# Recurrence steps queued behind dense products, with new step costs and finer dense pieces, in a two-layer hybrid decoder kernel

## The chip, the core and the metric

The kernel runs on one core of one Trainium2 chip. The metric is the device time of one execution in microseconds, the median over runs; lower is better. The five instruction streams of the core are named as in the profile: PE (TensorE; PEld is its weight loads), DVE (VectorE), ACT (ScalarE), POOL (GpSimd) and SP (SyncE, here only DMA issues).

## The reference

One inference step of a decoder with two layers, for a prompt of 2048 rows and for 8 sequences of 4 new rows each (the 32 sample rows, which bring their own past). Layer 0 is one input projection that feeds 4 heads of HGRN2 (a gated linear recurrence, "A") and 4 heads of forgetting attention ("B", or fox, with a paged cache), then one output projection. Layer 1 is GLA ("C"): the same kind of recurrence with 4 heads, key width 128 and value width 256. Cut to what matters here:

```python
def even_mixer(h, ...):                       # layer 0
    qa, fa, ia, ga, qb, kb, vb, gb, fb = split(h @ w_in)
    f = lb + (1.0 - lb) * sigmoid(fa)
    o_a, s_a = gated_linear_chunked(qa, 1.0 - f, ia, log(f), hgrn_s0)
    o_a = head_rmsnorm(o_a) * silu(ga)
    o_b = fox_attend(qb, kb, vb, log_sigmoid(fb + b)) * silu(gb)
    return concatenate([o_a, o_b]) @ w_out, s_a
def odd_mixer(h, ...):                        # layer 1
    q, k, v, g, r = split(h @ w_in)
    log_f = log_sigmoid(r @ w_gate + b_gate) / 16
    o, s = gated_linear_chunked(q * 128 ** -0.5, k, v, log_f, gla_s0)
    return (head_rmsnorm(o) * silu(g)) @ w_out, s
def step(S, chunk):                           # gated_linear_chunked, per chunk
    b = cumsum(log_f)
    o = (q * exp(b)) @ S + (scores of q and k, decayed by exp(b_t - b_s), causal) @ v
    S = S * exp(b_last) + (k * exp(b_last - b)).T @ v
```

with x + mixer(rmsnorm(x)) around each layer and a last rmsnorm.

## The kernel before

The prompt is worked on in two halves of 1024 rows; the first half (hf 0) carries the 32 sample rows along. The program has three stretches: layer 0 of both halves (to about 850 us of the trace), the attention of B over prompt and cache (to about 1260 us), and layer 1 with both output projections and the final norm.

**Dense work.** A projection is a sum over eight 128-row pieces of the contraction, each piece in three half-precision products (high by high, high by low, low by high; `mm3`, lines 626 to 628). `proj_fm` makes 24 products per result tile in PSUM, `proj_tm` 48 (two row tiles of 24). Each tile is then evacuated by ACT and DVE. The weights arrive by DMA (`wr_...`), and ACT, DVE and POOL scale and split them into halves (`w_...`, lines 356 to 364); `staged` spreads these steps over the units of 256 output columns that are traced.

**Recurrences.** `lin_attn` (line 690) is a generator, called sixteen times: 4 heads by 2 halves by 2 layers. Its parts in order, with the names that the profile shows:
- diagonal scores of 32 rows (`gd_`, L702) and, in hf 0, those of the sample rows (`gds_`, L707);
- the first product of q with the decay f on DVE (L711);
- seven levels w = 1, 2, 4, ... 64: score products on PE (`gl_`, L757; `gls_`, L777, for the sample rows), their way into the scores by DVE or ACT (L768, L764), then q times f on DVE (L789), k times f on POOL (L790) and f times f on DVE (L791). The next level's PE products read the new q and k;
- in hf 0 the `decode` part for the sample rows, put between the levels 4 to 64: `ktS_`, `kpad_`, `oS_` (products with the 8 old states), `stS_` (L841, new states), with the state times its decay on POOL (`s_`, L843) and a sum on DVE (L845);
- transposes of k (`kt_`, L869), states and outputs per chunk (`st_`, `o_`, L897 to L912), splits into two parts for layer 1 (`parts`, L861 on ACT, L862 on DVE or POOL), norm and gate (`finish`, L720 to L740) with the transposes `py_` (L729).

**What sets the order.** The Python program is traced from top to bottom, and a scheduler puts the traced instructions of each engine into one fixed queue, with its own estimate of when each can start; an instruction that is traced later can therefore be ordered earlier. `issue_after(x)` makes what is traced inside it stay behind instruction x in that order. Two generators are woven by `mux(a, ta, b, tb)`: each step yields a cost, and the one with the smaller share of its declared total is advanced. A recurrence is woven with two or three dense units in this way. The declared totals are `LIN_E` (layer 0, per half), `LIN_O` (layer 1) and `LIN3_B` (the last recurrence, woven with the output projection of hf 0); the steps' costs are the numbers that `lin_attn` yields. Layer 1's first three recurrences are also woven with `prep(1)`, which normalizes the rows of the second half (`x1r`: squares on ACT L567, times a gain row on POOL L569, ACT L574, times the row's factor on DVE L575).

## Time and profile before

| | us |
|---|---|
| median of 3 runs | 2328.9 (2323.44 to 2330.65) |
| the profiled execution | 2327.16 |
| its span in the trace | 2325.5 |
| PE busy | 2251.2 (97%) |
| DVE, ACT, POOL busy | 1377.3, 1026.8, 727.0 |
| granted TensorE clock, mean | 0.991 |

The span is what the trace records of the core; the execution's own time is 1.7 us longer. "Busy" counts matmuls until their modelled end, and successive matmuls overlap, so 97% does not mean that 3% is all that could be won. In the table of waits a row names the engine and the instruction that waited, then the engine and instruction that it waited for, and the total, number and longest of these waits. In the timeline a row gives start, duration, engine, line, the tiles written and read, and, in brackets, the idle time ahead of it and what ended it.

In the trace the eight recurrences of layer 0 lie between 95 and 830 us, those of layer 1 between 1470 and 2215 us.

### The profile page before, as it was taken

Reading aid. Unit: us, or ns where it says so; the run is one execution under the profiler, and the core shown is the slowest. Engines: PE = TensorE matmul, PEld = TensorE weight load, DVE = VectorE, ACT = ScalarE, POOL = GpSimd, SP = SyncE. Lnnn points to the kernel's source line nnn. Section 1 sums busy time; section 2 is a strip of 40 time slices with the busy share of each in tenths; the row PEclk is TensorE's granted clock in tenths of the full one; section 3 lists DMA queues with packets and bytes.
Section 4 is the critical chain, followed back from the end, with each engine's and each line's share of the span. In section 5 each row is a group of like instructions: output and inputs, shape, how many; then the busy total and the mean of one; then the engine's idle time right before and its main releaser. Section 6 shows DMA issues by size and latency. Waiting matters only on the chain.

```text
span 2325.5 us, 57677 instructions
## 1 busy us (share of the span) xinstructions
PE 2251.2 (97%) x23060; PEld 1605.5 (69%) x23060; DVE 1377.3 (59%) x3074; ACT 1026.8 (44%) x2264; POOL 727.0 (31%) x780
## 2 busy tenths in 40 slices
PE   7999999999999999999999999999999999999998
PEld 5677678855755876655446888777677666666887
DVE  7756558525653657577767455366665655547554
ACT  6434354211212226456656543545544644554343
POOL 2223424001201214123335445144551432222232
PEclk9999999999999999999999999999999999999999
DMA  7343444755432378876972969424224431115553
GB/s 238 121 126 99 146 135 163 206 137 160 143 120 73 124 187 282 236 248 191 274 257 82 343 193 267 130 79 143 82 93 93 124 92 58 49 56 164 171 186 150
DMA packets 357422, 361.63 MB, mean 156 GB/s; under 512 B 105777, under 2 KB 300658, under 8 KB 353058
## 3 DMA queue, kind: packets, MB, share of 16 engines
q1 hardware_dynamic: 355010, 351.33, 49.3%
q0 software_dynamic: 2144, 6.62, 0.8%
q8 instruction: 181, 2.97, 0.5%
q14 instruction: 87, 0.71, 0.1%
HBM read 244.54 MB, written 96.42 MB: 147 GB/s over the span
## 4 chain that ended last, share of the span: by engine, by line
PE 42%; DVE 2%; POOL 2%; ACT 2%; DMA 1%; issue 1%; SPq 0%; POOLq 0%; DVEq 0%; ACTq 0%
PE pt_o L626 4%; PE pt_o L627 4%; PE pt_o L628 4%; PE pt_Cv L626 2%; PE pt_Cv L628 2%; PE pt_Cv L627 2%; PE gl_C L757 1%; PE o_C L910 1%; PE pt L1449 1%; PE pv L1711 1%; DMA yr<-yT 1%; POOL s_C L843 1%; PE py_C L729 1%; POOL kC L790 0%; PE fo L626 0%
## 5 line engine op out<-in xcount | busy, mean ns | idle before, releaser
L626 PE MATMUL pt_o<-w_o,act 128*128 128x256 f16 x1024 | 279.6, 273 | 2.7 <-ACT sg1C L683 2.7
L627 PE MATMUL pt_o<-w_o,act 128*128 128x256 f16 x1024 | 279.7, 273 | 0.0
L628 PE MATMUL pt_o<-w_o,act 128*128 128x256 f16 x1024 | 279.5, 273 | 0.1
L626 PEld LDWEIGHTS <-act 128*128 128x128 f16 x2304 | 226.3, 98 | 37.4 <-issue 3.7
L627 PEld LDWEIGHTS <-act 128*128 128x128 f16 x2304 | 226.4, 98 | 32.9 <-issue 4.2
L628 PEld LDWEIGHTS <-act 128*128 128x128 f16 x2304 | 226.4, 98 | 30.6 <-issue 2.0
L790 POOL TENSOR_TENSOR kA<-kA,fA 128x512 f32<-128x512 f32 (+1 forms) x56 | 77.2, 1378 | 339.5 <-PE gl_A L757 274.5
L626 PE MATMUL pt_Cv<-w_Cv,act 128*128 128x256 f16 (+1 forms) x512 | 141.4, 276 | 0.0
L627 PE MATMUL pt_Cv<-w_Cv,act 128*128 128x256 f16 (+1 forms) x512 | 141.3, 276 | 0.0
L628 PE MATMUL pt_Cv<-w_Cv,act 128*128 128x256 f16 (+1 forms) x512 | 141.3, 276 | 0.0
L1429 POOL TENSOR_SCALAR L<-L,nm 128x512 f32<-128x512 f32 (+3 forms) x160 | 99.3, 634 | 107.7 <-DVE nm L1425 41.5
L1421 ACT ACTIVATE L<-L,nm,kc 128x512 f32<-128x512 f32 (+3 forms) x160 | 118.2, 740 | 27.7 <-DVE nm L1419 26.9
L790 POOL TENSOR_TENSOR kC<-kC,fC 128x512 f32<-128x512 f32 (+1 forms) x56 | 80.2, 1433 | 142.2 <-PE gl_C L757 100.1
L1456 ACT ACTIVATE th<-pt 128x512 f16<-128x512 f32 (+3 forms) x159 | 81.8, 529 | 92.5 <-PE pt L1449 91.1
L1457 DVE TENSOR_TENSOR tl<-pt,th 128x512 f16<-128x512 f32 (+3 forms) x159 | 95.1, 609 | 21.2 <-ACT th L1456 19.5
L1449 PE MATMUL pt<-ident,L 128*128 128x128 f32 x544 | 91.8, 281 | 1.6 <-POOL L L1429 1.0
L1573 PEld LDWEIGHTS pkt<-ident,pgcache_fox_k 128*128 128x128 f32 x512 | 58.3, 141 | 44.0 <-issue 25.1
L789 DVE TENSOR_TENSOR qC<-qC,fC 128x512 f32<-128x512 f32 (+1 forms) x56 | 73.4, 1311 | 23.4 <-PE gl_C L757 23.4
L1449 PEld LDWEIGHTS pt<-ident,L 128*128 128x128 f32 x544 | 67.6, 144 | 26.1 <-DVE tl L1457 5.2
L1573 PE MATMUL pkt<-ident,pgcache_fox_k 128*128 128x128 f32 x512 | 77.7, 278 | 6.8 <-ACT kts L1577 2.5
L1911 ACT ACTIVATE vC<-pt_Cv,kc 128x512 f32<-128x512 f32 (+1 forms) x40 | 23.9, 599 | 136.5 <-PE pt_Cv L628 136.5
L789 DVE TENSOR_TENSOR qA<-qA,fA 128x512 f32<-128x512 f32 (+1 forms) x56 | 70.1, 1253 | 12.5 <-PE gl_A L757 12.4
(959 smaller groups left out, 6558.2 us busy)
## 6 DMA issues: line engine op xcount, KB each, us to landing
pgcache_fox_k<-in_cache_fox_k SPq DMA_DIRECT2D x128, 256.0 KB, 4.2
pgcache_fox_v<-in_cache_fox_v SPq DMA_DIRECT2D x128, 256.0 KB, 4.1
yr<-yT SPq DMA_DIRECT2D x16, 1024.0 KB, 6.8
x1d<-xo SPq DMA_DIRECT2D x44, 256.0 KB, 3.6
wr_o<-in_w_out_even SPq DMA_DIRECT2D x32, 256.0 KB, 5.1
xo<-in_x_prompt SPq DMA_DIRECT2D x32, 256.0 KB, 5.6
wr_Cv<-in_w_in_odd SPq DMA_DIRECT2D x32, 256.0 KB, 3.5
x1r<-x1d SPq DMA_DIRECT2D x16, 512.0 KB, 4.2
```

The lines of the kernel that those rows point to most:

```text
L626: nc.tensor.matmul(ps, lh[0], rh[0], start=first, stop=False)
L627: nc.tensor.matmul(ps, lh[0], rh[1], start=False, stop=False)
L628: return nc.tensor.matmul(ps, lh[1], rh[0], start=False, stop=last)
L789: nc.vector.tensor_tensor(xv[:, :, 1], xv[:, :, 1], t0.to_broadcast([P, nb, w]), ALU.mult)
L790: nc.gpsimd.tensor_tensor(kv[:, :, 0], kv[:, :, 0], t1.to_broadcast([P, nb, w]), ALU.mult)
L1421: self.last_exp = nc.scalar.activation(lt[:, :w], lt[:, :w], AF.Exp, bias=nm[:, 0:1], scale=ib, accum_out=nm[:, 2 + j : 3 + j])
L1429: nc.gpsimd.tensor_scalar(lt[:, :w], lt[:, :w], nm[:, 1:2], 2.0**14, ALU.mult, ALU.mult)
L1449: nc.tensor.transpose(pt[:, w : w + P], rows[b][s // 4][0][:, (s % 4) * P : (s % 4 + 1) * P], self.ident)
L1456: nc.scalar.activation(th[:, a:w], pt[:, a:w], AF.Copy),
L1457: nc.vector.tensor_tensor(tl[:, a:w], pt[:, a:w], th[:, a:w], ALU.subtract)))
L1573: last = nc.tensor.transpose(pk[:, j * P : (j + 1) * P], pgs[j][:, h * P : (h + 1) * P], self.ident)
L1911: r = nc.scalar.activation(v[h][:, g : g + cnt], ps[:, :, :256], AF.Copy, scale=c)
```

## The change

Four things are altered together.

1. `beside_dense` takes the place of `mux` where a recurrence is woven with dense units. Each step of the recurrence is traced inside `issue_after` on the last product of the dense group traced so far (`self.dense_mm`), so that none of the step's instructions may be ordered ahead of it.
2. While `beside_dense` runs, `proj_fm` and `proj_tm` hand back control every twelve products or every 6 (`proj_fm` after 6, 12, 18 and 24 products of its 24; `proj_tm` after each 12 of its 48) instead of after each tile. These handbacks are of the type `Piece`, which `staged` passes on without counting them among the tiles that trigger its weight steps.
3. The costs that `lin_attn` yields are new: 2000 instead of 1000 behind `gd_`; 200 instead of 1000 behind a level's products and a new 2800 behind its three multiplications; 15000 instead of 5000 as the total of the levels against the decode part; 1200 instead of 440 behind `kt_` of layer 0; about 1000 behind each group of `st_` and `o_`.
4. The declared totals follow: `LIN_E` (20000, 15000) to (42300, 35500), `LIN_O` (31000, 23000) to (55500, 45000), `LIN3_B` 27000 to 52800.

The core of the diff:

```diff
-LIN_E = (20000.0, 15000.0)
-LIN_O = (31000.0, 23000.0)
-LIN3_B = 27000.0
+LIN_E = (42300.0, 35500.0)
+LIN_O = (55500.0, 45000.0)
+LIN3_B = 52800.0
...
+class Piece(float):
+
+    pass
...
     def proj_fm(...):
             ps = pps.tile([P, 512], F32, tag="pj", name=f"pf_{nm}{c0}")
+            full = 24 * (n / 2.4 + 3)
             for k in range(KT):
-                self.mm3(...)
+                self.dense_mm = self.mm3(...)
+                if self.fine and k in (1, 3, 5):
+                    yield Piece(full / 4)
             evac(ps[:M, :n], c0, n)
-            yield 24 * (n / 2.4 + 3)
+            yield full / 4 if self.fine else full
...
     def proj_tm(...):
                 for k in range(KT):
-                    self.mm3(...)
+                    self.dense_mm = self.mm3(...)
+                    if self.fine and (k == KT // 2 - 1 or k == KT - 1 and j + 1 < len(grp)):
+                        yield Piece(12 * 110)
             evac(ps[:n, : len(grp)], g, len(grp), n)
-            yield 24 * len(grp) * 110
+            yield (12 if self.fine else 24 * len(grp)) * 110
...
     def lin_attn(...):
         nc.vector.copy_predicated(dg, self.mdiag.unsqueeze(1).to_broadcast([P, 8, 32]), ps)
-        yield 1000
+        yield 2000
...
-                yield 1000
+                yield 200
                 if hf == 0 and w <= 2:
...
                 nc.vector.tensor_tensor(t1, t1, t0, ALU.mult)
+                yield 2800
...
-            yield from mux(decode(), DEC, levels(LEVELS[2:]), 5000.0)
+            yield from mux(decode(), DEC, levels(LEVELS[2:]), 15000.0)
...
-                yield 440
+                yield 1200
...
-            yield cpb * (1.25 if split else 1.7) * dv
+            yield 1000
...
-                yield (2.95 if split else 3.4) * dv
+                yield 1000 if split else 900
...
-                drain(mux(lin(0), LIN_E[hf], dense(3, 5), 2 * cost))
+                drain(self.beside_dense(lin(0), LIN_E[hf], dense(3, 5), 2 * cost))
...
+    def beside_dense(self, lin, t, dense, td):
+
+
+        def pinned():
+            while True:
+                with self.tc.issue_after(self.dense_mm.ins):
+                    c = next(lin, None)
+                if c is None:
+                    return
+                yield c
+
+        self.fine = True
+        yield from mux(pinned(), t, dense, td)
+        self.fine = False
...
-            for n, c in enumerate(us[j][1](self.ready.pop(j))):
+            n = -1
+            for c in us[j][1](self.ready.pop(j)):
+                if isinstance(c, Piece):
+                    yield c
+                    continue
+                n += 1
...
-                return mux(lins[hf](h), LIN_O[hf], dense(a, a + 3), 66000.0)
+                return self.beside_dense(lins[hf](h), LIN_O[hf], dense(a, a + 3), 66000.0)
...
-            drain(mux(lins[1](3), LIN3_B, third(), 88000.0))
+            drain(self.beside_dense(lins[1](3), LIN3_B, third(), 88000.0))
```

No instruction of work is added or taken away; the change moves instructions within the queues. Line numbers after it are 5 to 11 higher in these functions (L711 is then L721, L790 is L800, L843 is L854).

In the order of the queues the recurrences of layer 0's second half and of layer 1's second half, the last one excepted, stand almost as before. The four of each first half and the last one are moved. Two places follow.

POOL, first recurrence of layer 1 (`kC` is k times f for a level, its form gives the level: 128x128x4 is w = 4; `s_C` is an old state times its decay). Before:

```order
L790 TENSOR_TENSOR kC_21384<-kC_21384,fC_21484 128x128x4
L843 TENSOR_TENSOR s_C_22051<-s_C_22051,fC_21484 128x512
L843 TENSOR_TENSOR s_C_22053<-s_C_22053,fC_21484 128x512
L843 TENSOR_TENSOR s_C_22169<-s_C_22169,fC_21484 128x512
L843 TENSOR_TENSOR s_C_22171<-s_C_22171,fC_21484 128x512
L790 TENSOR_TENSOR kC_21384<-kC_21384,fC_21484 128x64x8
L790 TENSOR_TENSOR kC_21384<-kC_21384,fC_21484 128x32x16
```

After:

```order
L800 TENSOR_TENSOR kC_21384<-kC_21384,fC_21484 128x128x4
L854 TENSOR_TENSOR s_C_22101<-s_C_22101,fC_21484 128x512
L854 TENSOR_TENSOR s_C_22103<-s_C_22103,fC_21484 128x512
L800 TENSOR_TENSOR kC_21384<-kC_21384,fC_21484 128x64x8
L854 TENSOR_TENSOR s_C_22219<-s_C_22219,fC_21484 128x512
L854 TENSOR_TENSOR s_C_22221<-s_C_22221,fC_21484 128x512
L800 TENSOR_TENSOR kC_21384<-kC_21384,fC_21484 128x32x16
```

The k multiplication of level 8 moves ahead of the second pair of decays. The same is found in the second and third recurrence of layer 1. On PE the products of level 8 and of level 16 (`gl_C`) are then separated by 34 dense products of `pt_Cv` with a `stS_C` and the second half of `oS_C`; before, by 17 of them, two `stS_C` and ten of the short sample products `pS_Cv`.

DVE, second recurrence of layer 1, from the diagonal scores (L703, after it L713) to the first level (L768, then L778). `w_Cg` is a weight split, `sg1C` the gate of the dense unit before, `rst_n` and `x1r` belong to the normalization of rows, `scTs` takes `gds_C`, and `qC` with 128x1056 is the first product with f. Before:

```order
L703 COPY_PREDICATED dg<-mdiag,gd_C_23012 128x256
L357 SCALAR_TENSOR_TENSOR w_Cg_23360<-wr_Cg_22804,kc,w_Cg_23360 128x512 x2
L685 SCALAR_TENSOR_TENSOR sg1C_22924<-th_C_23008,sg1C_22924 128x352
L431 TENSOR_SCALAR rst_n_23111<-nss_23109 128x1
L431 TENSOR_SCALAR rst_n_23486<-nss_23484 128x1
L708 COPY_PREDICATED scTs_880<-mdiag,gds_C_23116 32x128
L711 TENSOR_TENSOR qC_22342<-qC_22342,fC_22574 128x1056
L575 SCALAR_TENSOR_TENSOR x1r_22812<-x1r_22812,rsr_n_23113 128x1024
L575 SCALAR_TENSOR_TENSOR x1r_23106<-x1r_23106,rsr_n_23488 128x1024
L768 COPY_PREDICATED dg<-mlev_819,gl_C_23120 128x128
```

After:

```order
L713 COPY_PREDICATED dg<-mdiag,gd_C_23025 128x256
L362 SCALAR_TENSOR_TENSOR w_Cg_23376<-wr_Cg_22850,kc,w_Cg_23376 128x512 x2
L695 SCALAR_TENSOR_TENSOR sg1C_22937<-th_C_23021,sg1C_22937 128x352
L718 COPY_PREDICATED scTs_880<-mdiag,gds_C_23086 32x128
L721 TENSOR_TENSOR qC_22312<-qC_22312,fC_22519 128x1056
L436 TENSOR_SCALAR rst_n_23168<-nss_23166 128x1
L436 TENSOR_SCALAR rst_n_23460<-nss_23458 128x1
L778 COPY_PREDICATED dg<-mlev_819,gl_C_23090 128x128
```

The first product with f moves ahead of the two `rst_n`, and the two `x1r` products move behind the first level. On PE, in the first three recurrences of layer 1, `gds_C` then stands 24 dense products behind `gd_C` (before 48), and the first `gl_C` 36 behind `gds_C` (before 34), so that the first level comes 22 products earlier.

More of the change, by code (lines that the diff above doesn't have):

```diff
@@ L147, in consts @@
         nc.vector.memset(self.mhalf, -0.5)
-        self.col = col
+        self.col, self.fine = col, False
         self.g_even = col("g_even", i["norm_even"][0], KT)
```

14 lines of the change are left out of this document (7 added, 7 removed).

## The prediction

> **What bounds the kernel now.** I read the busy times first, then the waits of PE, then the stretches, and last the timeline at each wait. PE sets the end. This is its line on the profile's page:
>
> ```profile
> PE 2251.2 (97%) x23060; PEld 1605.5 (69%) x23060; DVE 1377.3 (59%) x3074; ACT 1026.8 (44%) x2264; POOL 727.0 (31%) x780
> ```
>
> The change adds no product, so it can act on the time only through the moments in which PE has nothing to do or switches between kinds of products. The windows of the stretches show where these moments are (columns: window, its length, then busy time and count of each engine, granted clock, DMA):
>
> ```profile
> 95.00:430.00 335.00, 328.72 (x4113) 244.32 (x4112) 211.15 (x455) 131.62 (x314) 111.86 (x87) 0.99 0.42 134
> 500.00:830.00 330.00, 329.37 (x3652) 210.96 (x3651) 176.29 (x416) 73.40 (x193) 48.80 (x43) 1.00 0.39 124
> 850.00:1260.00 410.00, 383.65 (x2685) 222.19 (x2683) 288.87 (x918) 232.68 (x539) 143.58 (x263) 0.98 0.75 231
> 1470.00:1840.00 370.00, 359.77 (x4254) 261.56 (x4253) 227.26 (x404) 194.69 (x404) 154.06 (x119) 0.99 0.35 102
> 2120.00:2215.00 95.00, 90.50 (x1213) 77.95 (x1212) 58.03 (x104) 34.66 (x82) 26.86 (x22) 0.98 0.59 187
> ```
>
> PE idles 0.6 us beside the four recurrences of layer 0's second half, 6.3 beside those of its first half, 10.2 beside the four of layer 1's first half and 4.5 beside the last one. The attention's 26 us are in a stretch where no recurrence runs. So about 21 us are all that the edit can reach, and these are its waits, from the list of PE's waits (total, times, longest):
>
> ```profile
> PE gl_C L757 <- POOL kC L790: 5.6, 4, 1.8
> PE pt_o L626 <- ACT sg1C L683: 2.7, 1, 2.7
> PE gl_C L757 <- DVE qC L711: 1.9, 1, 1.9
> PE pt_Bk L626 <- DVE Bvs L1071: 1.9, 1, 1.9
> PE o_C L626 <- ACT pd_C01s L861: 1.6, 1, 1.6
> PE kt_C L869 <- ACT scT L764: 1.4, 1, 1.4
> PE stS_A L841 <- DVE kpad_A L818: 1.3, 1, 1.3
> PE gl_A L757 <- POOL kA L790: 0.7, 1, 0.7
> ```
>
> **Step 1, the k multiplication behind four decays.** POOL in the first recurrence of layer 1, and PE around the level that waits for it, from the timeline:
>
> ```profile
> 1538.78 1.72 POOL L790 TENSOR_TENSOR kC<-kC,fC 128x512 f32<-128x512 f32 x1
> 1540.46 5.28 POOL L843 TENSOR_TENSOR s_C<-s_C,fC 128x512 f32<-128x512 f32 x4
> 1545.70 1.14 POOL L790 TENSOR_TENSOR kC<-kC,fC 128x512 f32<-128x512 f32 x1
> ```
>
> ```profile
> 1541.44 0.74 PE L757 MATMUL gl_C<-qC,kC 128*32 128x16 f32 x64
> ...
> 1543.78 0.27 PE L627 MATMUL pt_Cv<-w_Cv,act 128*128 128x256 f16 x1
> 1543.89 0.27 PE L628 MATMUL pt_Cv<-w_Cv,act 128*128 128x256 f16 x1
> ...
> 1546.89 0.72 PE L757 MATMUL gl_C<-qC,kC 128*32 128x16 f32 x63 [1.74 <-POOL kC L790]
> ```
>
> Level 8's products are over at 1542.2, but POOL works on decays until 1545.74 and finishes the k of that level at 1546.84. PE had run out of other work 1.74 us earlier. The same happens in the second and third recurrence (the waits of these three make 5.2 of the 5.6). With the multiplication ahead of the second pair of decays, POOL is free at 1540.46 + 2 × 1.32 = 1543.1, so the new k is there at 1544.3, about 2.5 us earlier. On PE the next level comes later instead: dense products start 0.11 apart (1543.78 to 1543.89), 34 of them now lie between the two levels and take 3.7 us beside the state products. Arrival moves from 1545.1 to about 1546.5, and the wait is gone with some 2 us to spare. A wait costs a little more than its idle time, since the product ahead is counted until its modelled end, 0.27 after its start, while the next would have started after 0.11: 0.16 each. Gain: 5.2 + 3 × 0.16 = **5.7 us**. The second pair of decays is now late by one multiplication, 1.1 us; who waits for it is the sum on DVE (L845) and a store, not PE. Cover for the level after it (16): both pairs lie ahead of its multiplication as before, and the fourth recurrence keeps its wait of 0.4. Bounds: nothing gained if other work in the new places delays POOL by over 2 us, and 5.9 at most.
>
> **Step 2, the first level comes 22 dense products earlier** in these three recurrences, 22 × 0.11 = 2.4 us. What it needs is the first product of q with f on DVE. The timeline of DVE in the first, second and third recurrence, and POOL in the second:
>
> ```profile
> 1521.34 2.67 DVE L685 SCALAR_TENSOR_TENSOR sg1C<-th_C,sg1C 128x352 f32<-128x352 f32 x1
> ...
> 1524.00 0.28 DVE L708 COPY_PREDICATED scTs<-mdiag,gds_C 32x128 f32<-32x128 int8 x1
> 1524.19 1.24 DVE L711 TENSOR_TENSOR qC<-qC,fC 128x1056 f32<-128x1056 f32 x1
> ```
>
> ```profile
> 1611.23 2.70 DVE L685 SCALAR_TENSOR_TENSOR sg1C<-th_C,sg1C 128x352 f32<-128x352 f32 x1
> ...
> 1615.14 0.15 DVE L431 TENSOR_SCALAR rst_n<-nss 128x1 f32<-128x1 f32 x1 [1.15 <-ACT nsq L567]
> 1615.21 0.28 DVE L708 COPY_PREDICATED scTs<-mdiag,gds_C 32x128 f32<-32x128 int8 x1
> 1615.41 3.25 DVE L711 TENSOR_TENSOR qC<-qC,fC 128x1056 f32<-128x1056 f32 x1
> ```
>
> ```profile
> 1706.21 2.70 DVE L685 SCALAR_TENSOR_TENSOR sg1C<-th_C,sg1C 128x352 f32<-128x352 f32 x1
> ...
> 1709.09 1.24 DVE L711 TENSOR_TENSOR qC<-qC,fC 128x1056 f32<-128x1056 f32 x1
> ```
>
> ```profile
> 1611.20 2.35 POOL L569 TENSOR_TENSOR x1r<-x1r,grow 128x1024 f32<-128x1024 f32 x1 [0.44 <-ACT nsq L567]
> ...
> 1615.19 2.35 POOL L569 TENSOR_TENSOR x1r<-x1r,grow 128x1024 f32<-128x1024 f32 x1 [0.49 <-ACT nsq L567]
> ```
>
> Beside POOL's x1r multiplication the gate takes 2.70 and the q product 3.25, and they end 0.4 and 1.1 us after POOL does (1613.55, 1617.54); alone the q product takes 1.24. [...]
>
> The gate's operation over all its uses (least, median and longest ns):
>
> ```profile
> L685 DVE SCALAR_TENSOR_TENSOR sg1C<-th_C,sg1C x20: 518/683/2703, 1510.9 to 2135.6; 128x352 f32<-128x352 f32 x12, 128x512 f32<-128x512 f32 x8
> ```
>
> PE in the first recurrence, the sample scores among dense products, and in the second, for its arrival:
>
> ```profile
> 1522.60 0.27 PE L628 MATMUL pt_Cv<-w_Cv,act 128*128 128x256 f16 x1
> 1522.81 0.25 PE L707 MATMUL gds_C<-qC,kC 128*32 128x32 f32 x2
> 1522.99 0.28 PE L626 MATMUL pt_Cv<-w_Cv,act 128*128 128x256 f16 x1
> ...
> 1612.81 0.25 PE L707 MATMUL gds_C<-qC,kC 128*32 128x32 f32 x2
> ```
>
> First recurrence: PE reached the level at 1522.99 + 34 × 0.11 = 1526.7 and will reach it at 1524.3; the q product ends at 1525.4. A wait of 1.0 is new, and the second level's wait of 0.3 for DVE goes. Second: PE arrived at 1616.7 and waited until 1618.7. It will arrive at 1614.3. DVE is done with the gate at 1613.9, and the q product no longer stands behind the second `rst_n`, which waited for ACT until 1615.14. If it starts at 1614.2, a microsecond before POOL's second multiplication, it ends at 1615.4: a wait of 1.2 for 1.9. If it meets it, up to 1618.7, a wait of 4.4. I take 1.3, since nothing ahead of it on DVE waits for ACT any more. Third: in the new order no x1r work stands on POOL there, so the gate takes 0.5 to 0.7 and the product is over before 1709, while PE arrives at 1709.3 (3.1 behind the gate's start, as in the second): nothing. Sum: +1.0 − 0.3 − 0.6 = **+0.1 us**, bounds −1.9 (all waits go) and +8 (rival A).
>
> **Step 3, the last recurrence** is woven with the output projection; its later levels come 3 to 5 us later on PE and its first transposes 6.6 us later. ACT there:
>
> ```profile
> 2162.31 0.72 ACT L362 ACTIVATE wr_o<-wr_o,kc 128x512 f32<-128x512 f32 x1 [4.78 <-DMA wr_o<-in_w_out_odd]
> 2164.50 0.72 ACT L362 ACTIVATE wr_o<-wr_o,kc 128x512 f32<-128x512 f32 x1 [1.47 <-DMA wr_o<-in_w_out_odd]
> 2165.23 0.77 ACT L764 ACTIVATE scT<-gl_C 64x256 f32<-64x256 f32 x2
> ```
>
> The scores' copy stood behind a weight scaling that waited for its transfer. With the transposes 6.6 us later the copy is over before PE comes: **−1.6 us** (1.4 and the 0.16). A weight split on POOL is now ahead of the k of level 16 instead of level 32; its 0.4 us of wait stays. The wait of 2.7 at the start of that stretch (`pt_o` for a gate on ACT) is ahead of the recurrence's first step and stays.
>
> **Step 4, layer 0's first half.** The third recurrence's `stS_A` now stands behind all eight `oS_A` and two dense products, about half of its 1.3 goes; in the fourth, the first level's 0.7 goes, since its products come 1.5 us later. Gain **1.5 us** with the 0.16s. Against that, the fourth's state and output steps move 1 to 4 us later, into the evacuation of `Bk` and `Bv` on DVE, where PE waits 1.9 today; there the waits may shift by 2 either way, and I take 0.
>
> **Step 5, switches.** The order has 17 more changes between dense and recurrence products. Around `gds_C` above the next dense product starts 0.39 after the last one, instead of 0.11, with two products of 32 rows between them: some 0.1 us per switch is lost at most. **+1.5 us**, bounds 0.5 and 3. The wait of `o_C` for `pd_C01s` stays at 1.6: ACT's order there is the same. In the attention, which the edit doesn't touch, a few instructions change place; 0, bounds ±3.
>
> Sum: −5.7 + 0.1 − 1.6 − 1.5 + 1.5 = −7.2 us. Profiled execution 2327.16 − 7.2 = 2320.0. The median of the runs is 1.7 above that execution, so the forecast for the median is 2321.7, rounded to **2321.5 us**.
>
> **Rivals.** A, *the wait only moves to the first level.* The three first levels come 2.4 us earlier, and in the first two the q product meets a POOL multiplication of x1r, which costs it 2.0 more (3.25 against 1.24), while in the third the gate still meets one: waits of 3.0, 4.4 and 1.0 instead of 0, 1.9 and 0, together +6.5 − 0.3 instead of +0.1. The time is then 2321.7 + 6.1 = 2328, no change. For it: DVE is packed there from the weight split to the q product. Against it: fewer x1r steps lie there in the new order.
>
> B, *step 1 gains only half.* POOL's queue is in order; if x1r or a weight split gets between, or PE's other work before level 16 shrinks, each wait falls to 0.9 rather than to 0: −2.9 instead of −5.7, and the time is 2324.5. For it: POOL's k multiplication of 1.72 at 1538.78 shows that it too is lengthened by DVE. Against it: 2 us of margin.
>
> C, *slower: a step that is pinned can't fill a dense wait any more.* Place: layer 0's first half, where DVE is busy 63% (211.15 of 335.00) and the dense tile waits for its evacuation, as `pt_Bk` for `Bvs` does. Today the scheduler may slip a ready recurrence step in front of such a tile; pinned, the step stands behind the stalled product, and its DVE work follows late too. Each time costs the 1.9 of that row. It decides once over four such waits arise beyond today's one: −7.2 + 4 × 1.9 is about 0; with eight of them the time is 2321.7 + 15.2 = 2337. Against it: the recurrences of the second half, whose order is nearly the same, wait only 0.6 us in all, so the even spread is mostly present there already.
>
> D, *the order moves too little to show.* 8 of 16 recurrences hardly move, the others' waits are traded for others of like size: 2328 to 2330.
>
> **How the numbers follow.** This forecast 0.52, A 0.12, B 0.14, C 0.14, D 0.08. About 0.3% (7.0 us) is what a measurement of this kernel can tell from no change, so faster means below 2321.9 and slower above 2335.9. The forecast's own range is 2312 to 2327: the bounds of steps 2, 4 and 5 and the attention's 3 together make 5 to 6 either way, and it reaches further down because the 21 us of waits leave more to gain in places that I set to 0 than there is to lose. Two thirds of it lie below 2321.9: 0.35. B adds a quarter of its chance and A a tenth, 0.05: faster 0.40, and slower 0.12 from C with over seven more waits or with other mishaps of its kind, within 0.3% 0.48. The range for 8 in 10 takes in B, A and D and half of C: 2311 to 2334.
>
> **What would show it.** Right: no `gl_C` wait for `kC` in the first three recurrences of layer 1 (the row falls from 5.6 to about 0.5); `kt_C` for `scT` gone; `gl_C` for `qC` at L721 between 1.5 and 3 us in two waits; PE idle in 1470 to 1840 down from 10.2 to about 5. A shows as the last row with 6 us or more; B as a `kC` row of about 3; C as more and longer waits of `pt_Bk`, `pt_Bv` or `pf_B` for DVE before 430. The forecast fails if a wait outside these places changes by more than 3 us, in the attention above all.

## The result: 0.21% slower, and the profile after

| | before | after |
|---|---|---|
| median of 21 runs each | 2325.93 | 2329.51 |
| lowest and highest | 2320.26 to 2332.46 | 2323.61 to 2336.48 |
| the profiled execution | 2327.16 | 2330.60 |
| its span | 2325.5 | 2328.9 |

The ratio of after to before is 1.0021, with a 95% interval from 1.0013 to 1.0029: about 5 us slower, inside the 0.3% that I had called no change, and clearly not the forecast gain of 7. Ratios here compare undisturbed runs on the same chip, and so need not equal the quotient of the two medians. The changed kernel in a second set of runs, later, gave 1.0035 (1.0023 to 1.0048).

The page's line of busy times after the change:

```profile
PE 2246.7 (96%) x23060; PEld 1603.3 (69%) x23060; DVE 1368.6 (59%) x3074; ACT 1028.0 (44%) x2264; POOL 722.6 (31%) x780
```

PE's work is the same 23060 products. Its idle time rose from 74.3 to 82.2 us. The stretches of the prediction, after (window, length, busy time and count of PE, PEld, DVE, ACT, POOL, clock, DMA):

```profile
95.00:430.00 335.00, 324.46 (x4089) 241.42 (x4087) 208.30 (x453) 131.35 (x313) 111.47 (x87) 0.99 0.42 134
...
1470.00:1840.00 370.00, 360.04 (x4263) 262.51 (x4262) 224.70 (x406) 196.04 (x406) 149.21 (x119) 0.99 0.36 105
2120.00:2215.00 95.00, 92.67 (x1229) 79.17 (x1227) 54.03 (x101) 36.26 (x85) 26.06 (x22) 0.98 0.57 182
```

Beside layer 0's first half PE now idles 10.5 us instead of 6.3. Beside layer 1's first half it idles 10.0 instead of 10.2, where I had expected about 5. Beside the last recurrence it idles 2.3 instead of 4.5, as hoped. The list of PE's waits after the change, for the places of the prediction:

```profile
PE gl_C L767 <- DVE rst_n L436: 3.9, 2, 2.9
PE pt_o L631 <- DVE xo L1889: 3.8, 1, 3.8
...
PE pf_Bg L631 <- DVE Bq L1037: 3.3, 2, 2.0
...
PE pt_Bv L631 <- DVE Bvs L1082: 2.3, 1, 2.3
...
PE zC L1982 <- ACT qC L1996: 1.6, 1, 1.6
...
PE pt_Bk L631 <- DVE Bvs L1082: 1.3, 1, 1.3
...
PE py_C00S L739 <- ACT scT L774: 1.3, 1, 1.3
PE py_C01S L739 <- ACT scT L774: 1.3, 1, 1.3
...
PE gl_A L767 <- POOL kA L800: 1.2, 1, 1.2
PE o_C L631 <- ACT pd_C01s L872: 1.2, 1, 1.2
```

The row that I aimed at, `gl_C` for `kC` with 5.6, is gone altogether; so is `kt_C` for `scT`. In their place stand rows that were not there: `pt_o` for `xo`, `pf_Bg` for `Bq`, `zC`, `py_C00S`, a longer `py_C01S` and a longer `pt_Bv`. (The first row names `rst_n`; the level waits for the q product just ahead of it on DVE, as shown below.)

Where the 3.4 us between the two profiled executions arose follows from the starts of the same dense products in both traces, after minus before:

| at (us) | after − before | since the row above |
|---|---|---|
| 462, behind layer 0's first half | +2.9 | +2.9 |
| 1276, behind the attention | +0.75 | −2.2 |
| 2078, behind seven recurrences of layer 1 | −0.76 | −1.5 |
| 2216, end of the last recurrence | −2.1 | −1.3 |
| 2243, 27 us later | +3.5 | +5.6 |

The first two rows are shaky, because they rest on one profile of the kernel before. Against it the attention is 0.4 to 5.9 us shorter in all sixteen other traces of this case. At 462 the four kernels below whose layer 0 has the old order stand at +1.2 to +2.5 as well, with one stretch more of half clock (3.41 us), and the eight with the changed layer 0, this one among them, at +0.6 to +4.5. So of layer 0's +2.9 only a part, and perhaps little, comes from the change. The last row is firm: from 2216 to 2243 the four other traces in which layer 0 and the last recurrence are both changed (one of them without the pin) lose 5.4 to 6.5, the one with layer 0 undone loses 3.7, and the four with the old last recurrence lose nothing.

So most of step 1's gain was eaten within layer 1, layer 0 lost up to 2.9, and 5.6 were lost just behind the last recurrence, in a place that the prediction did not look at.

**Layer 1, the loss at the recurrences' other end.** POOL in the first recurrence does what step 1 said:

```profile
1537.98 1.71 POOL L800 TENSOR_TENSOR kC<-kC,fC 128x512 f32<-128x512 f32 x1
1539.66 2.65 POOL L854 TENSOR_TENSOR s_C<-s_C,fC 128x512 f32<-128x512 f32 x2
1542.28 1.59 POOL L800 TENSOR_TENSOR kC<-kC,fC 128x512 f32<-128x512 f32 x1
```

The k multiplication runs between the two pairs of decays, and three waits of 1.7 to 1.8 end. At the second recurrence's first level, DVE and POOL:

```profile
1612.89 2.72 DVE L695 SCALAR_TENSOR_TENSOR sg1C<-th_C,sg1C 128x352 f32<-128x352 f32 x1
1615.53 0.28 DVE L718 COPY_PREDICATED scTs<-mdiag,gds_C 32x128 f32<-32x128 int8 x1
1615.73 3.20 DVE L721 TENSOR_TENSOR qC<-qC,fC 128x1056 f32<-128x1056 f32 x1
...
1612.87 4.95 POOL L574 TENSOR_TENSOR x1r<-x1r,grow 128x1024 f32<-128x1024 f32 x2 [0.45 <-ACT nsq L572]
```

POOL's two x1r multiplications, which were 1.6 us apart before, now run back to back for 4.95 us: the small factor between them (`rsr_n`) moved behind, and ACT's squares, for which the second of them waited before (0.49), come earlier. Beside them both the gate (2.72; the median of its 20 uses, in two shapes, is 0.61) and the q product (3.20; the median of eight is 1.23) are long; PE comes 22 products earlier, 2.4 us, and waits 2.9. Two kernels of the experiments bear this out: with finer pieces alone, and in the best version below, the two multiplications are 1.6 us apart again, the q product takes 1.24, and no first level waits over 1.0. Each of DVE's two operations ends only after one of POOL's two: the gate at 1615.61, 0.4 after POOL's first (1615.23), the q product at 1618.93, 1.1 after the second (1617.81). Why DVE takes longer beside POOL there, these runs don't show.

The end of the recurrences on ACT, two rows from the first recurrence and six from the second:

```profile
1560.87 0.72 ACT L367 ACTIVATE wr_Cv<-wr_Cv,kc 128x512 f32<-128x512 f32 x1 [4.04 <-DVE qC L799]
1561.49 0.75 ACT L774 ACTIVATE scT<-gl_C 64x256 f32<-64x256 f32 x2
...
1653.68 0.75 ACT L367 ACTIVATE wr_Cv<-wr_Cv,kc 128x544 f32<-128x544 f32 x1 [5.47 <-DMA wr_Cv<-in_w_in_odd]
1654.34 0.53 ACT L1996 ACTIVATE qC<-pf_C02q,kc 128x352 f32<-128x352 f32 x1
1654.78 1.14 ACT L579 ACTIVATE x1r<-x1r,rsr_n 128x1024 f16<-128x1024 f32 x1
1655.81 0.76 ACT L774 ACTIVATE scT<-gl_C 64x256 f32<-64x256 f32 x2
1657.04 0.75 ACT L367 ACTIVATE wr_Cv<-wr_Cv,kc 128x544 f32<-128x544 f32 x1 [0.47 <-DMA wr_Cv<-in_w_in_odd]
1657.69 0.40 ACT L872 ACTIVATE pd_C01s<-scT 128x256 fp32r<-128x256 f32 x1
```

In the second recurrence a weight scaling waits 5.47 us for its transfer, and behind it on ACT stand an evacuation (`zC` waits 1.6 for it), an x1r step, the score copy (`py_C01S` waits 1.3) and a split (`o_C` waits 1.2). Before, ACT stood still at the same weight for 4.60, and only `o_C` with 1.6 and `py_C01S` with 0.2 felt it. In the first recurrence the score copy for which `py_C00S` waits 1.3 stands behind a weight scaling too, ahead of which ACT idled 4.04. I put this down to the 15000 against which the decode part is paced: the sample rows' norm and transposes are stretched to the end of the recurrence, next to the dense tile's end, so more of PE's work stands behind this moment. The run with 9000 below bears that out for the transposes.

**Layer 0.** ACT around the evacuations of `Bq`, before:

```profile
324.23 1.02 ACT L1025 ACTIVATE Bq<-pf_Bq,kc 128x352 f16<-128x352 f32 x2
```

ACT and DVE after:

```profile
322.26 0.57 ACT L1036 ACTIVATE Bq<-pf_Bq,kc 128x352 f16<-128x352 f32 x1
...
326.83 1.15 ACT L533 ACTIVATE xhl<-ny,rsr_n 128x1024 f16<-128x1024 f32 x1 [2.96 <-POOL rsr_n L438]
...
328.88 0.98 ACT L1036 ACTIVATE Bq<-pf_Bq,kc 128x352 f16<-128x352 f32 x2
...
329.53 1.04 DVE L1037 SCALAR_TENSOR_TENSOR Bq<-pf_Bq,kc,Bq 128x352 f16<-128x352 f32 x2
```

Before, two evacuations of `Bq` ran one behind the other. Now the second stands on ACT behind a normalization of rows, in which ACT is idle for 2.96 us until POOL has its factor, and behind the eight instructions of a recurrence's norm (four squares and their sums, 1.0 us from 327.89 on). PE, which needs the PSUM tile, waits 2.0. At the like place of another recurrence, at 162.6, it waits 1.3; there the evacuation stands behind the norm's instructions alone, and these wait for PE's `o_A`.

**Behind the last recurrence.** The chain that ended last runs there through a load of y, whose row starts at 2224.44:

```profile
2220.71 2.73 DVE act L1846 x4
...
2224.44 7.34 DMA yr<-yT
...
2234.04 0.67 DVE xo L1889
2234.75 0.27 PE pt_o L631
```

The load of the next piece of y waits for a buffer, which is free when DVE has split the piece before. DVE came to that late, because of this operation:

```profile
2213.47 0.75 DVE L1889 SCALAR_TENSOR_TENSOR xo<-pt_o,kc,xo 128x512 f32<-128x512 f32 x1 [7.71 <-DMA xo<-x1d]
```

It waited 7.71 us for a residual tile. SP's issues say why, first after the change, then before:

```profile
2202.16 0.37 SPq L1832 DMA_DIRECT2D yr<-yT  x1
...
2205.35 0.44 SPq L1888 DMA_DIRECT2D xo<-x1d  x1
```

```profile
2196.55 1.71 SPq L1857 DMA_DIRECT2D xo<-x1d  x2
...
2202.73 0.37 SPq L1801 DMA_DIRECT2D yr<-yT  x1
...
2220.09 0.41 SPq L1801 DMA_DIRECT2D yr<-yT  x1
```

Before the change the residual loads stood ahead of the y load in SP's queue. Now the y load stands ahead of one of them: SP held it until 2202.16, issued nothing in the 5.6 us behind the store ahead of it, and the residual load followed at 2205.35, 7 to 9 us later than before. The same operation of DVE before the change, and ACT's first split of the y piece before and after:

```profile
2209.57 0.75 DVE L1858 SCALAR_TENSOR_TENSOR xo<-pt_o,kc,xo 128x512 f32<-128x512 f32 x1 [2.64 <-PE pt_o L628]
```

```profile
2228.70 2.56 ACT L1814 ACTIVATE act<-yr,kc 128x512 f16<-128x512 f32 x4 [6.29 <-DMA yr<-yT]
```

```profile
2231.87 2.56 ACT L1845 ACTIVATE act<-yr,kc 128x512 f16<-128x512 f32 x4 [11.54 <-DMA yr<-yT]
```

DVE's operation is 3.9 us late, the next y load 4.35 us late (2224.44 for 2220.09), and ACT's split of that piece 3.2 us. PE, which before had no idle time from 2215 to 2240, waits 3.8. The lateness is not all of it. In each of the eleven traces in which PE waits at this place, it resumes 2.9 us after ACT's first split of the piece (here 2231.87 and 2234.75). Before, that moment (2231.6) lay only 1.4 us ahead of PE (2232.95). So the y piece's 3.2 us and the 2.1 us that PE itself had gained by then add up, less the 1.4: 3.9, against 3.8 measured.

### The profile page after: what moved, and what is told of

It is laid out like the page before. It is cut to its first block, busy times and chain, and to the rows that moved or that the text cites. A ratio compares the mean times of both kernels' runs of the same rounds, so it can differ in the third digit from the quotient of the medians.

```text
span 2328.9 us, 57652 instructions
## 1 busy us (share of the span) xinstructions
PE 2246.7 (96%) x23060; PEld 1603.3 (69%) x23060; DVE 1368.6 (59%) x3074; ACT 1028.0 (44%) x2264; POOL 722.6 (31%) x780
## 4 chain that ended last, share of the span: by engine, by line
PE 41%; DVE 3%; ACT 2%; DMA 2%; issue 1%; SPq 1%; POOL 0%; POOLq 0%; DVEq 0%; ACTq 0%
PE pt_o L631 4%; PE pt_o L633 4%; PE pt_o L632 4%; PE pt_Cv L631 2%; PE pt_Cv L633 2%; PE pt_Cv L632 2%; PE gl_C L767 1%; PE o_C L921 1%; PE pt L1480 1%; DMA yr<-yT 1%; PE pv L1742 1%; PE py_C L739 1%; PE fo L631 1%; PE fo L632 0%; DMA wr_Cv<-in_w_in_odd 0%
## 5 line engine op out<-in xcount | busy, mean ns | idle before, releaser
L800 POOL TENSOR_TENSOR kA<-kA,fA 128x512 f32<-128x512 f32 (+1 forms) x56 | 77.7, 1388 | 331.4 <-PE gl_A L767 268.7
L800 POOL TENSOR_TENSOR kC<-kC,fC 128x512 f32<-128x512 f32 (+1 forms) x56 | 85.1, 1520 | 131.4 <-PE gl_C L767 92.9
```

The source lines that it names most:

```text
L800: nc.gpsimd.tensor_tensor(kv[:, :, 0], kv[:, :, 0], t1.to_broadcast([P, nb, w]), ALU.mult)
```

## The experiments

The kernel was rebuilt from the changed one with a switch for each stretch of recurrences: `p` pins the steps, `f` makes the dense pieces fine, `c` takes the new costs and totals, `d` the new decode total. With all letters it is the changed kernel, with none its instructions have the order of the kernel before. All of these kernels do the whole computation.

```diff
+PARTS_E = ("pfcd", "pfcd")
+PARTS_O = ("pfcd", "pfcd")
+PARTS_L = "pfcd"
...
-        yield 2000
+        yield 2000 if 'c' in self.parts else 1000
...
-            yield from mux(decode(), DEC, levels(LEVELS[2:]), 15000.0)
+            yield from mux(decode(), DEC, levels(LEVELS[2:]), 15000.0 if 'd' in self.parts else 5000.0)
...
+                if "p" in parts:
+                    with self.tc.issue_after(self.dense_mm.ins):
+                        c = next(lin, None)
+                else:
+                    c = next(lin, None)
...
-        self.fine = True
-        yield from mux(pinned(), t, dense, td)
+        self.fine, self.parts = "f" in parts, parts
+        yield from mux(pinned(), t["c" in parts], dense, td)
```

`PARTS_E` is layer 0 (first half, second half), `PARTS_O` layer 1's first seven recurrences (same), `PARTS_L` the last one. Ratios below are to the kernel before, with 95% intervals; the changed kernel's is 1.0021.

### Which stretch loses

```diff
-PARTS_L = "pfcd"
+PARTS_L = ""
```

> Only the last recurrence (woven with the output projection) goes back to the old weave, costs and whole tiles; everything else is the changed kernel. Theory 1 (the loss arises at the end): the SP queue of the changed kernel has the load of a residual tile xo behind the yr load that waits for stores of y, DVE's evacuations come late, and PE waits 3.8 us at 2231 and then runs 3 us at half rate (1.6 us more). Then that 5.5 us goes, the old waits of the last recurrence (0.4 and 1.4, with what belongs to them 2.1) come back: about 3.4 us below the changed kernel, so level with the kernel before within 1.5 us. Theory 2 (the loss is spread over the recurrences, the end varies by chance): within 1 us of the changed kernel, 3 to 4 us above the one before.

Measured 1.0007 (0.9993 to 1.002). PE's longest wait from 2120 to 2240 us; the two others there, of 0.9 and 0.3, are not for `xo` either:

```profile
PE pt_o L634 <- ACT sg1C L696: 2.2, 1, 2.2
```

By the difference from 1.0021 the last stretch costs 0.14%, 3.3 us. The two intervals overlap, so the ratios alone don't show it; the trace does, in which nothing is lost from 2216 to 2243. Now layer 0:

```diff
-PARTS_E = ("pfcd", "pfcd")
+PARTS_E = ("", "")
```

> All eight recurrences of layer 0 go back to the old weave, costs and whole tiles; layer 1 is that of the changed kernel. Theory 4: the dense tiles of layer 0's first half wait because their evacuations on ACT and DVE stand behind more of the recurrence's work (pf_Bg for Bq 3.3, pt_Bv for Bvs 2.3, first level 1.2 in the changed kernel): 3 to 4.3 us below the changed kernel. Rival: these waits are traded for others in the attention that follows: within 1 us.

Measured 1.0007 (0.9994 to 1.002); `pf_Bg` for `Bq` is gone and the waits of the kernel before are back (`pt_Bk` 1.9, `pt_Bv` 0.8, `stS_A` 1.3). By the same reckoning layer 0 costs another 0.14%, and here the traces don't make it firmer (see the table of starts). With both undone:

```diff
-PARTS_E = ("pfcd", "pfcd")
-PARTS_L = "pfcd"
+PARTS_E = ("", "")
+PARTS_L = ""
```

> The change in layer 1's first seven recurrences alone; layer 0 and the last recurrence as in the kernel before. If the losses of layer 0 (theory 4) and of the end (theory 1) add, it is 6 to 7 us below the changed kernel, that is about 2 us below the one before (ratio 0.999): the three waits for kC are gained (5.7) and some 4 us of it are given back in the new waits of the same recurrences. Rival: the losses are not additive, chance in the attention and at the end decides: ratio 1.0005 or more.

Measured 0.999 (0.9976 to 1.0003). Taken at their middles the three shares add up: layer 1's first seven recurrences win some 2 us, the other two stretches lose 3.3 each. The repeat of the changed kernel itself, with no edit, served to see whether these shares stand on a solid sum:

> The changed kernel itself, beside the same runs of the kernel before as the two that follow. If its first ratio of 1.0021 holds here, the parts taken out one by one (1.0000 to 1.0007) are each worth 0.14 to 0.2%; if it comes at 1.0005 or less, most of these differences lie between the sessions and not in the parts.

It gave 1.0035 (1.0023 to 1.0048), so the loss is real and perhaps larger than the first 0.21%, though the two intervals meet; `xo` waited 4.4 in it. Each share above is therefore known to about 0.15% only, which is its own size.

### What makes the wait behind the last recurrence

In the changed kernel the load of y's second piece is kept behind the residual load:

```diff
+        for n, steps in enumerate(self.y_pieces(hf, layer, act, pool)):
+            if (hf, layer, n) == (1, 1, 1):
+                with self.tc.issue_after(self.xos[1, 2, 6].ins):
+                    steps.pop(0)()
...
-                    nc.sync.dma_start(t[:m, :cnt], src)
+                    self.xos[layer, u, g] = nc.sync.dma_start(t[:m, :cnt], src)
```

> The changed kernel, with one DMA order altered on SP: the load of the second yr piece of the second half is kept behind the load of the residual tile xo of the third output unit. Theory 1: that load is the first link of the chain, so the wait of PE for xo (3.8 us) and the half rate behind it go while the gains in the last recurrence stay: 5.5 us below the changed kernel, 2 us below the one before. Rival: the splits of y on DVE, which stand ahead of the evacuation, are late by themselves, since y is stored later; then the wait stays at 3 us or more and the time within 1 us of the changed kernel, or above it, since yr starts later.

Measured 1.0001 (0.999 to 1.0013). The wait is halved:

```profile
PE pt_o L634 <- DVE xo L1899: 1.9, 1, 1.9
```

DVE's operation no longer waits for a residual tile there but for PE, and no slowing of the clock follows (1.00 from 2215 to 2290 us, against 0.98 in the changed kernel). Measured against PE's own progress, the split of y's piece starts 1.9 us earlier than in the changed kernel. So the late residual load is about half of the wait. Two more edits, to the last recurrence of the changed kernel: new costs without pin and pieces, and pieces alone.

```diff
-PARTS_L = "pfcd"
+PARTS_L = "c"
```

> The changed kernel, but the last recurrence has only the new costs: whole tiles, no pin. On SP the load of the residual tile xo then stands ahead of the yr load again. Theory 1 with theory 6: PE's wait for xo at 2231 falls below 1.5 us and the half rate behind it is gone, while kt_C for scT stays gone: 4 to 5.5 us below the changed kernel, level with the one before or below it. Rival: the new costs alone make DVE late there: the wait stays at 2 us or more.

```diff
-PARTS_L = "pfcd"
+PARTS_L = "f"
```

> The changed kernel, but the last recurrence has only the pieces of twelve: old costs and total, no pin. On SP the yr load then stands ahead of the xo load, as in the changed kernel. If the pieces are the cause of the wait at the end, it is there: PE waits for xo 2 us or more at 2231, ratio 1.001 to 1.003 (the run with the costs alone in this place had 1.0000, the one with neither 1.0007). Rival: the wait needs the new costs too: gone here, ratio below 1.0005.

Costs alone: 1.0000 (0.9984 to 1.0015), a wait of 2.0, though its residual load is ahead of the y load. Pieces alone: 1.0001 (0.9986 to 1.0016), a wait of 1.2, though its residual load is behind. In the run with layer 0 undone the whole change is there and the two loads stand as in the changed kernel, yet the wait was 2.0, too. So neither SP's order nor one part of the change decides alone. What the traces have in common is whether DVE stood still for the residual tile: in the five with 7.4 to 8.1 us of it, PE waited 3.5 to 4.4 there, in all others 2.0 or less.

The other half is the sum told above, less a late residual load. With layer 0 undone, ACT's split is 0.4 us earlier than before the change and PE 3.8 us; less the 1.4 that is 2.0. With costs alone, the split is 1.4 later and PE 2.0 earlier, again 2.0. PE ran into a transfer that had only just been hidden, and what it had gained ahead of this place was lost here.

### Which part of the change harms

New costs and decode total everywhere, without pin and pieces:

```diff
-PARTS_E = ("pfcd", "pfcd")
-PARTS_O = ("pfcd", "pfcd")
-PARTS_L = "pfcd"
+PARTS_E = ("cd", "cd")
+PARTS_O = ("cd", "cd")
+PARTS_L = "cd"
```

> The changed kernel with the new costs and totals alone: nothing pinned, whole tiles of 24 and 48 products. Theory 6: the pieces of twelve do the harm, since a recurrence step is then traced inside a tile, ahead of that tile's evacuation; then pf_Bg for Bq in layer 0 and the wait for xo at 2231 go, and the time is 5 us or more below the changed kernel, below the one before. Rival: the costs do it: ratio about 1.002 as in the changed kernel.

Measured 1.0035 (1.002 to 1.005), against my expectation. The waits are others, and longer:

```profile
PE py_C L742 <- ACT wr_o L370: 4.8, 1, 4.8
PE py_C00S L742 <- ACT scT L777: 3.9, 1, 3.9
```

With whole tiles of 24 or 48 products, I think, the new costs place recurrence steps in large lumps. At any rate the same costs with the pieces, in the kernel without the pin below, come to 1.0005, so the pieces repair more than they harm. Pieces everywhere, all else as before:

```diff
+PARTS_E = ("f", "f")
+PARTS_O = ("f", "f")
+PARTS_L = "f"
```

> The kernel before with one thing altered: the dense tiles hand back every 6 or 12 products while a recurrence runs; old costs and totals, no pin. Theory 6 after the run with the costs alone (1.0035): neither part alone gains; the pieces put the yr load ahead of the xo load at the end (wait at 2231 of 2 us or more) and the evacuation of Bq behind the recurrence's norm (pf_Bg for Bq or Bg 2 us or more), and the three waits for kC stay, as POOL keeps the four decays together: ratio 1.001 to 1.004. Rival: the pieces are harmless and only the costs move evacuations: within 0.001 of 1.

Measured 0.9991 (0.9979 to 1.0003): no harm, perhaps 2 us of gain; `gl_C` for `kC` falls from 5.6 to 1.9. And the changed kernel without the pin (`"fcd"` in all five places):

> The changed kernel without the pin: the new costs, totals and pieces stay, issue_after on the last dense product is left out. In the order of the queues this moves some 30 rows of PE in all recurrences together (the rest differs in the attention alone). Theory 8: the pin does nothing for the time, costs and pieces make the whole effect: ratio 1.001 to 1.003, with the same waits (xo 3 to 4 us at 2231, pf_Bg for Bq 3.3, first level 2.9). Rival: the pin holds steps back and makes the losses: ratio below 0.9995.

Measured 1.0005 (0.9992 to 1.0018), with the large waits of the changed kernel to the tenth, that of the first levels (3.9) among them:

```profile
PE pt_o L634 <- DVE xo L1896: 3.8, 1, 3.8
...
PE pf_Bg L634 <- DVE Bq L1041: 3.3, 2, 2.0
```

Only `pt_Bv` for `Bvs` falls from 2.3 to 0.2, while `pt_Bk` has 1.7 instead of 1.3. The pin moves some 30 of 23060 PE instructions, at the end of layer 0's fourth recurrence and at a few places behind it, and none in the last recurrence. Whether it costs nothing or up to 0.3% these runs don't settle.

### Rates: prep and the decode total

If the first levels wait because of x1r work, a slower pace of `prep` in the changed kernel should help:

```diff
-            drain(mux(prep(1), 10000.0, three(0, 11), 240000.0))
+            drain(mux(prep(1), 10000.0, three(0, 11), 288000.0))
```

> The changed kernel, with the total that the normalization of the second half's rows (x1r) is woven against raised from 240000 to 288000, as the recurrences' costs rose by that share, so that this work returns to its old pace. Theory 3: the x1r work, which the new costs brought forward, makes the new waits in layer 1 (first level of the second recurrence 2.9, py_C00S 1.3, py_C01S 1.3, zC 1.6): they go for the most part, 4 us below the changed kernel. Rival: the recurrences' own new places make them: no change within 1 us, and the same rows stay.

Measured 1.0048 (1.0031 to 1.0064), the worst of all: `gl_C` for `rst_n` rose to 4.9, `zC` to 3.5 and `py_C00S` to 2.8. At the second recurrence it changed nothing: POOL's two multiplications still run back to back (4.94), the q product takes 3.20, and PE waits 2.9. So this run doesn't test the cause there; the two kernels named above, with the multiplications apart, speak for it. Elsewhere x1r steps came to stand in worse places. A middle value of the decode total in the changed kernel:

```diff
-            yield from mux(decode(), DEC, levels(LEVELS[2:]), 15000.0)
+            yield from mux(decode(), DEC, levels(LEVELS[2:]), 9000.0)
```

> The changed kernel with the total of the levels against the decode part at 9000 instead of 15000. The sample outputs' transposes py_C00S then come 33 dense products earlier on PE, ahead of zC instead of beside it; POOL keeps the k multiplication between the pairs. Theory 7: the decode part, stretched by 15000 up to the recurrence's last level, makes py_C00S and py_C01S wait (1.3 each) and zC (1.6): about 4 us below the changed kernel, ratio 1.0005 or less. Rival: the last levels, which now stand beside zC themselves, take these waits over: ratio 1.0015 or more.

Measured 1.0029 (1.0015 to 1.0043): the `py_C` waits left, but the last levels came late instead (`kt_C` for `kC` 1.8, `gl_C` for `fC` 1.8) and `zC` rose to 3.0. Now the smallest edit that brings step 1's order on POOL, in the kernel before: the decode total alone, in layer 1's first half alone.

```diff
-            yield from mux(decode(), DEC, levels(LEVELS[2:]), 5000.0)
+            yield from mux(decode(), DEC, levels(LEVELS[2:]), 6000.0 if 'd' in self.parts else 5000.0)
...
+PARTS_E = ("", "")
+PARTS_O = ("d", "")
+PARTS_L = ""
```

> The kernel before, with one number altered: in layer 1's first half the total of the levels that the decode part is woven against is 6000 instead of 5000. On POOL this puts the k multiplication of level 8 between the two pairs of state decays, as the whole change does, and moves almost nothing else (no pin, no pieces, old costs). Theory 5: the three waits of 1.7 to 1.8 us go and nothing comes for them: 5.2 to 5.9 us below the kernel before, ratio 0.9975. Rival: the order brings its own new wait (the sample outputs come later), as in the whole change: within 1 us of the kernel before.

Measured 0.9974 (0.9959 to 0.9989). PE's waits from 1516 to 1800 us:

```profile
PE gl_C L770 <- DVE qC L802: 2.7, 2, 1.6
PE o_C L634 <- ACT pd_C01s L876: 1.6, 1, 1.6
PE gl_C L770 <- POOL kC L803: 0.7, 1, 0.7
```

The one number ends most of the waits that I aimed at: `kC` falls from 5.2 in this window to 0.7. At the recurrences' other end `zC`, `py_C00S` and `py_C01S` have 0.5 to 0.7 each, not 1.3 to 1.6. But `gl_C` for `qC` rises from 1.9 to 2.7, so that all waits in this window fall from 8.9 to 6.7 only, and with one stretch of half clock instead of two PE gains 3.4 us between 1500 and 1800. The measured 0.26% are 6 us; the rest isn't traced to a place. Pieces everywhere on top of it (`"f"` added in all five places):

> The kernel before with the pieces in all recurrences and, in layer 1's first half, the share of 6000; old costs and totals, no pin. The run with the share alone left waits of 3.0 (gl_C for qC) and 1.1 (for kC) in these recurrences, since the levels 8 and 16 are 12 dense products apart there; with the pieces they are 22 apart. If the two add: 1.5 to 3 us below the run with the share alone, ratio 0.996. Rival: the pieces give back elsewhere (layer 0, end): ratio 0.9975 or more.

Measured 0.9974 (0.996 to 0.9987): no further gain. In its trace layer 0 ends 3.2 us later than in that of the next kernel. Pieces and total in layer 1's first seven recurrences only:

```diff
+PARTS_E = ("", "")
+PARTS_O = ("fd", "f")
+PARTS_L = ""
```

> The same, with the pieces in layer 1's first seven recurrences alone; layer 0 and the last recurrence as in the kernel before. If the pieces cost something in layer 0 and at the end, this is the faster of the two: ratio 0.9955 to 0.9965. Rival: the pieces are harmless there: equal within 0.001.

Measured 0.9958 (0.9945 to 0.9972), median 2318.32 of 5 runs beside 2326.58: the best version found, about 10 us faster than before and some 15 faster than the change (its interval meets those of the two kernels above). PE's waits from 1516 to 1800 us:

```profile
PE gl_C L770 <- DVE rst_n L439: 2.8, 3, 1.0
```

With one of 0.9 and three of 0.3 or less, the waits in this window fall from 8.9 to 4.4 us. The clock adds to it: in the profile of before it stands at half twice in this window (3.41 us each, from 1547.7 and from 1619.4), here never: an estimated 3 us, from the 1.67 that one such stretch cost among dense products (last section). Together that is the 7.6 us that PE gains between 1500 and 1800 in this trace. The rest of the 10 us isn't traced to a place, since this kernel's profiled execution, with 2326.3, was the longest of its five (in it PE waited 2.4 us for a transfer at 1451 us that doesn't show in the profile of before).

## Why the prediction was wrong

**Step 1** (k multiplication behind four decays, −5.7) was right in mechanism: the three waits (5.2) ended, and POOL's rows stand in the order foreseen. With the decode total alone the kernel gained 6 us, but its trace places only 3.4 of them here, so the size isn't shown by itself.

**Step 2** (first levels earlier, +0.1) was right for the first recurrence (1.0 predicted and found) and the third (nothing), and off by size for the second: 2.9 instead of 1.3. I took the milder of two bounds because nothing on DVE ahead of the product waited for ACT any more. But that same freeing let POOL's two multiplications run back to back. Rival A had this mechanism; its place was one recurrence, not three. The clock, which no step counted, doesn't change the balance of this stretch: it stood at half twice before (from 1547.7 and 1619.4, behind the waits for `kC` and for `qC`) and twice after (from 1562.8 and 1658.4, behind `py_C00S` and behind `zC`, `py_C01S` and `o_C`).

**A term was missing: the other end of these recurrences.** I compared the front, where the change moves products earlier, and wrote that `o_C` keeps its 1.6 since ACT's order there is the same. ACT's order in the second recurrence was, but for one x1r step; PE's was not. `zC`, `py_C00S` and `py_C01S` came to wait for what stands behind the stalled weight scalings: +4.2 − 0.2 − 0.4 = +3.6 us. With step 2's error this is the 5 us of idle time that I expected to vanish and that stayed. By the runs the net of this stretch was −0.1%, not −0.25%.

**Step 3** (last recurrence, −1.6) was right about its wait, which is gone. The −1.3 at the recurrence's end doesn't show its size, since the kernel with the old last recurrence has −1.2 over the same stretch. And the step stopped there. Behind it PE came 2.1 us early to a y transfer that had been hidden by only 1.4, and this transfer came 3.2 late, behind a residual load that SP's order had delayed: 3.8 of wait and 1.7 of half clock. The prediction followed PE, DVE, ACT and POOL through the two orders, and never SP's issues, nor did it ask what PE would meet when it came earlier. This was the dearest miss: 0.14% by the run that takes it away, 5.6 us by the traces.

**Step 4** (layer 0, −1.5) had the wrong sign: PE's idle time there rose by 4.2, and the trace puts the loss at up to 2.9. Of the two waits that I counted one fell as supposed (`stS_A` from 1.3 to 0.6), the other rose (`gl_A` from 0.7 to 1.2, not to 0). And the sum left out that a norm's eight instructions, and in one place a row normalization that waits for POOL, would come on ACT between PE and the evacuation of `Bq` (+3.3). `Bk` and `Bv` shifted by +0.9 together, within my 2.

**Step 5** (17 more switches, +1.5) isn't seen. In layer 0 the loss of progress, 2.9, is smaller than the added idle time, 4.2, so no cost of the order beside its waits shows. No run isolates it.

**Rival C** named the right place for the loss in layer 0 (dense tiles waiting for their evacuation before 430 us) and the wrong cause. Without the pin the same `pf_Bg` waits are there to the tenth; only `pt_Bv` for `Bvs` (2.3 to 0.2) goes with the pin. It takes the new costs and the pieces together: with the costs alone `pf_Bg` for `Bq` waits 1.0, with the pieces alone not at all.

**The sum**: predicted −7.2. From the table of starts: −1.5 for layer 1's first seven recurrences instead of −5.6 and a part of the switches' 1.5, −1.3 for the last recurrence, then +5.6 behind it, +2.9 for layer 0 and −2.2 in the attention, where my ±3 held, by one profile each. The base was off, too: the median of 2328.9 came from three runs, that of 21 is 2325.93, so the forecast of 2321.5 lay 4.4 below it, not 7.4. The sentence that the forecast would fail if a wait outside the named places changed by more than 3 us came true with `xo`.

## What to carry to other kernels

When an edit moves work on one engine, compare the two orders of every engine's queue at the places where the moved work ends, not only where it starts: here SP's issues behind the last recurrence and ACT's evacuations, behind a late weight and behind a norm, made up most of the loss. Ask also how far ahead of PE the next transfer lands: a gain larger than that margin (1.4 us here) is lost there. A change with four parts should be split before it is judged: one number in one stretch gained 0.26% (0.9974), with finer pieces there 0.42% (0.9958, of five runs), while the same ideas applied everywhere lost 0.2 to 0.35%. And a wait of PE can cost more than its length: here one of 3.8 was followed by 3.41 us at half clock, 1.67 more.

## What the runs showed of the hardware

The granted TensorE clock fell to half (0.50) at some waits of PE, by the records of the clock in the traces for 3.41 us or twice that (6.83). In the changed kernel's profile, three windows, in, just behind and well behind the `xo` wait (columns as above; the clock is the third number from the end):

```profile
2230.50:2235.00 4.50, 0.67 (x19) 0.45 (x12) 2.38 (x4) 2.56 (x4) 0.00 (x0) 1.00 1.00 369
2235.30:2238.50 3.20, 3.20 (x17) 2.28 (x15) 0.72 (x2) 0.14 (x1) 0.00 (x0) 0.50 0.81 269
2239.00:2243.00 4.00, 4.00 (x39) 3.58 (x38) 3.82 (x7) 4.00 (x9) 1.22 (x1) 1.00 0.23 72
```

In 3.2 us only 17 products start, instead of some 30. Dense products stand 0.21 apart there instead of 0.11, and this costs 1.67 us on top of a wait of 3.8: 17 steps from start to start take 3.52 us there (2235.19 to 2238.71), and at 0.109 each they would take 1.85. In the 17 traces of this case, without the program's first 100 us, the attention and what comes after 2300 us, there are 63 such stretches, 48 of them single and 15 double. Each begins during a wait of PE or within 2 us behind one. All 9 waits of over 3.2 us had one, of those from 1.9 to 3.2 us 25 of 47, from 1.2 to 1.9 us 29 of 99, from 0.8 to 1.2 us 5 of 82; some of the shorter ones stand close to others, but the 1.3 of `py_C00S` at 1562 in the changed kernel stands alone. The 2.9 of `gl_C` at 1616 in the same kernel had none. What sets the clock, and why one wait brings it to half and another of the same length doesn't, the runs don't show. The prediction counted a wait at its idle time and 0.16; by these counts one of over 3.2 us in this kernel is to be counted at some 1.7 more, an estimate from the one stretch above, and one of 1.9 to 3.2 us at that in about half of the cases (25 of 47).
